# A mixture-of-experts stage: how the rows of each expert are gathered and turned, and which weight loads go first

## The chip, the cores and the metric

The kernel runs on one core of one Trainium2 chip. The core has five engines that run at the same time, each with its own list of instructions: TensorE (PE in the profile; PEld is its weight load), VectorE (DVE), ScalarE (ACT), GpSimd (POOL) and SyncE (SP), which here only issues DMA transfers. The metric is the device time of one execution in microseconds (us); lower is better.

## The reference

One layer of a hybrid encoder block for 512 tokens of width 1024, all in float32. A token mixer (chunked spatial gating beside a gated delta rule) comes first and isn't touched by the change. Then each token goes to 2 of 32 experts, chosen by a router, and each expert is a gated two-layer network:

```
h = _layer_norm(DEEPNORM_ALPHA * h + mix, ln1_g[l], ln1_b[l])
ffn = _hier_moe(h, w_rg[l], b_rg[l], w_re[l], b_re[l], w1[l], w3[l], w2[l])
h = _layer_norm(DEEPNORM_ALPHA * h + ffn, ln2_g[l], ln2_b[l])
...
def expert_block(args):
    xb, e = args
    hb = jax.nn.silu(xb @ w1[e]) * (xb @ w3[e])
    return hb @ w2[e]
```

`w1[e]` and `w3[e]` are 1024 x 512, `w2[e]` is 512 x 1024, so an expert has 6 MB of weights. With 1024 (token, expert) pairs on 32 experts, an expert has 32 rows on average.

## The kernel before, in words

Up to about 690 us of the trace the kernel runs the mixer. Towards its end, normalised rows are written to DRAM in `h1_dram`, two halves of a 128-row tile at a time, by DMAs on ACT's queue (line 978). The router makes for each expert its count of rows (`cnti`) and the list of its tokens (`idx`); the rank of a row is its place in that list. The lists have 160 places (`NB`): ranks 0 to 127 in the first column of `idx`, ranks 128 to 159 in the second (`sort`, line 1086).

From there `Experts.run` (its core stands below) goes through 32 blocks, one for each expert. The order of the work in this stage is written by hand: each engine executes its instructions in the order in which the code emits them.

- **Weights.** `load` issues 1 MB loads on SP's queue (line 395 for the first blocks, line 397 under the condition that the expert has rows): six for each expert, four for the first product and two for the second, 192 in all. They go round through 18 buffers (`raw`). A load waits until the buffer's former contents have been read. 18 loads are issued ahead of the first block; block b then issues four after its first pass and two after the second pass of block b-1.
- **Gathers.** `fetch` (line 1303) has POOL gather the rows of a block from `h1_dram` by two indirect DMAs: 128 rows into one buffer and 32 into another, always both. Two buffers of each kind alternate, and block b+2 is fetched at the start of block b.
- **Turning the rows.** `turn_x` (lines 1314 to 1329) has PE transpose the 128 gathered rows in 8 pieces of 128 columns, four into each of the PSUM banks `t0` and `t1`. ACT (line 1320) and DVE (line 1322) each take four pieces to `x` in SBUF and apply the gain and the bias of the normalisation. Ranks 128 to 159 are transposed (line 1326) only if the count is over 128, into the right half of the bank `yz`; DVE reads them from there in any case (lines 1328 and 1329).
- **First pass.** `up` (line 1342) multiplies x by the first four weight chunks into the bank group `u`: ranks 0 to 31 always in 32 matmuls, ranks 32 to 95 and 96 to 159 each behind a branch on PE with 16 wider ones (the profile counts every matmul in float32 twice, so 64, 96 or 128 for a first pass). `gate` takes silu on ACT (line 1349) and the product on DVE (line 1350) to h.
- **Second pass.** `turn` transposes h through `t1` and `t0` (lines 1356 and 1358; ACT copies them to `hT`, lines 1359 and 1360), and `down` (line 1370) multiplies hT by the last two chunks: ranks 0 to 31 into the left half of `yz`, the others into `y0` and `y1` behind branches. `store_y` copies the results out of PSUM (DVE for `yz`, line 1378; ACT for the others, line 1381) and POOL stores them.

The passes are interleaved: after the first pass of block b, PE transposes the rows of block b+1, runs the second pass of block b-1, and turns h of block b. Pieces of the router's bookkeeping (`more`) are dealt out between these steps. After the blocks come one loop for experts with over 160 rows, which has nothing to do for these inputs, the gather of results for each token, and the last normalisation.

Of the kernel before, what the change touches and what calls it, by code (L numbers as in the profile page):

```python
# [30 lines left out]
NP = 2  # L31
NB = 32 + 64 * NP
NX = 3
# [987 lines left out]
class Router:  # L1021
# [17 lines left out]
    def tile(self, t):  # L1039
# [38 lines left out]
        for i, (a, b) in enumerate(((0, 128), (128, NB))):  # L1078
            for k in range(2):
                nc.tensor.matmul(self.sps[i][0:b - a], oh[:, k, a:b], wt[:, k],  # L1080
                                 start=k == 0 and t == 0, stop=k == 1 and t == NT - 1)

    def sort(self):
        nc, v = self.nc, self.nc.vector
        for i, n in enumerate((128, NB - 128)):
            v.tensor_scalar(self.idx[0:n, i], self.sps[i][0:n], 2.0 * T, None, op0=OP.add)
# [95 lines left out]
    def overflow(self, W, ps, i):  # L1182
# [8 lines left out]
        for h, (a, b) in enumerate(((0, 128), (128, NB))):  # L1191
# [10 lines left out]
class Experts:  # L1202
# [8 lines left out]
    def __init__(self, kk, ctx, cst, land, h1_dram, y_dram):  # L1211
# [8 lines left out]

        self.y0 = ps.tile([128, 512], F32, name="yz")
        self.u = ps.tile([128, NP + 1, 512], F32, name="u")
        self.xt = self.ec(self.tile_pool(name="ext", bufs=2))
# [4 lines left out]
    def clear(self):  # L1228

        for t in [self.u[:, 0:NP], self.y0] + self.y:  # L1230
            self.nc.vector.memset(t, 0.0)

    def run(self, blocks, more=None, clear=None):
# [10 lines left out]
        def load(n):  # L1244
            for _, (b, c) in zip(range(n), todo):
                blk = blocks[b]
                if blk[5] and b not in conds:
# [52 lines left out]
    def fetch(self, b, i):  # L1300

        x = self.land[i][self.nland[i] % 2][0:(128, NB - 128)[i]]
        self.nc.gpsimd.indirect_dma_start(out=x, out_offset=None, in_=self.h1_dram,  # L1303
                                          in_offset=bass.IndirectOffsetOnAxis(ap=self.blocks[b][2 + i], axis=0),
                                          bounds_check=T - 1, oob_is_err=False)
        self.s[b].setdefault("r", []).append(x)
        self.nland[i] += 1

    def turn_x(self, b):

        nc, r, m = self.nc, self.s[b]["r"], NB - 128
        x = self.s[b]["x"] = self.xt.tile([128, KD, NB], F32, name="x")
# [3 lines left out]
        lc = self.kk.lc  # L1316
        for k in range(KD):
            src, lg, lb = self.t[k // 4][:, k % 4 * 128:k % 4 * 128 + 128], lc[:, 0, k:k + 1], lc[:, 1, k:k + 1]
            if k < 4:
                nc.scalar.activation(out=x[:, k, 0:128], in_=src, func=AF.Identity, bias=lb, scale=lg)  # L1320
            else:
                nc.vector.tensor_scalar(x[:, k, 0:128], src, lg, lb, op0=OP.mult, op1=OP.add)
        z = self.y0[:, 256:256 + KD * m]
        with self.tc.If(self.n(b) > 128):
            for k in range(KD):
                nc.tensor.transpose(z[:, k * m:k * m + m], r[1][:, k * 128:k * 128 + 128], self.cst["ident"][0:m, 0:m])
        xh = x[:, :, 128:NB]
        nc.vector.tensor_tensor(out=xh, in0=z.rearrange("p (k n) -> p k n", k=KD), in1=bc(lc[:, 0], m, 2), op=OP.mult)  # L1328
        nc.vector.tensor_tensor(out=xh, in0=xh, in1=bc(lc[:, 1], m, 2), op=OP.add)
# [64 lines left out]
def build(nc, tc, a):  # L1394
# [139 lines left out]
    def dynamic(oi, j):  # L1534
        ids = []

        def srcs():
            if not ids:
# [8 lines left out]
    blocks = [(e * NB, static(e), r.idx[:, 0, e:e + 1], r.idx[0:NB - 128, 1, e:e + 1], r.cnti[0:1, e:e + 1],  # L1547
               i > 3)
# [9 lines left out]
    with tc.For_i(0, nv, 1) as i:  # L1558
# [3 lines left out]
        ex.run([((i + E) * NB, dynamic(so, 0), idx[:, 0:1], idx[0:NB - 128, 1:2], so[0:1, 1, 0:1], False)])  # L1562
# [70 lines left out]
```

## Time and profile before

| what | value |
| --- | --- |
| median of 3 runs | 1276.2 us (1274.17 to 1276.59) |
| the profiled execution, its own time | 1277.76 us |
| its span, first to last instruction | 1276.1 us |
| mean granted clock of PE over the span | 0.951 |
| busy over the span: PE, DVE, ACT, POOL | 1082.8, 634.7, 494.4, 199.9 us |
| DMA traffic over the span | 300.23 MB, 235 GB/s |
| weight loads of the experts | 192 of 1024 KB, 20.6 us from issue to landing |

The busy times are sums over the whole span, of which the stage that the change touches is the part from 700 us on; inside it, a short stretch says more than the sum. A timeline row gives the start, the length, the engine, the line, what is written and read, how often, and in brackets the idle time before it with what ended it. PEclk is the clock granted to PE: 1 is 2.4 GHz, 0.5 is 1.2 GHz.

### The profile page before, as it was taken

The numbers are of one execution on the slowest core, as the hardware profiler recorded it, in microseconds if no ns is written. First come the engines' busy times: TensorE is split into PE (matmuls) and PEld (weight loads), VectorE is DVE, ScalarE is ACT, GpSimd is POOL, SyncE is SP. The second block draws the span as 40 slices with busy tenths as digits, with TensorE's granted clock in tenths as the row PEclk, the third lists the DMA queues.
The fourth block names the chain that finished last, engine by engine and source line by source line (L and its number), as shares of the span: only waits on it lengthen the run. The fifth ranks groups of instructions, "written<-read, shape, count | busy, mean of one in ns | idle before, by whom it ended". The sixth has DMA issues, their size and how long they took to land. (4 is left out here: it accounts for less than half of the span.)

```text
span 1276.1 us, 20920 instructions
## 1 busy us (share of the span) xinstructions
PE 1082.8 (85%) x7782; PEld 716.5 (56%) x7782; DVE 634.7 (50%) x1376; ACT 494.4 (39%) x1039; POOL 199.9 (16%) x367
## 2 busy tenths in 40 slices
PE   4999999999999999999999488878787777789820
PEld 2887788877777777768887234343434333334310
DVE  7475542468777777754764434442223232222256
ACT  6233552445454455445331324332424233222231
POOL 1000110022211212200000202111212212112033
PEclk9999999999999999999989699999999898898965
DMA  4422223699311120114673749999999999999833
GB/s 172 161 66 67 83 83 92 236 371 362 93 51 55 61 67 33 51 52 166 233 280 148 286 190 378 412 416 416 416 417 416 417 416 417 417 417 417 352 107 119
DMA packets 79997, 300.23 MB, mean 235 GB/s; under 512 B 12192, under 2 KB 37024, under 8 KB 55552
## 3 DMA queue, kind: packets, MB, share of 16 engines
q1 hardware_dynamic: 67536, 278.42, 56.6%
q0 software_dynamic: 9744, 15.10, 3.5%
q10 hardware_dynamic: 2592, 4.99, 1.1%
q8 instruction: 86, 1.41, 0.5%
q14 instruction: 39, 0.32, 0.1%
HBM read 285.48 MB, written 50.33 MB: 263 GB/s over the span
## 5 line engine op out<-in xcount | busy, mean ns | idle before, releaser
L1342 PE MATMUL u<-raw,x 128*32 128x256 f32 (+1 forms) x2496 | 226.2, 435 | 14.8 <-DMA raw<-in_w 14.4
L212 PE MATMUL psi<-hTh,hi 128*128 128x512 f32 x456 | 187.9, 414 | 2.2 <-ACT hi L212 2.2
L212 PE MATMUL psi<-hTh,lo 128*128 128x512 f32 x456 | 188.1, 414 | 0.3 <-DVE lo L212 0.3
L212 PE MATMUL psi<-hTl,hi 128*128 128x512 f32 x456 | 186.0, 410 | 0.0
L1350 DVE TENSOR_TENSOR h<-h,u 128x640 f32<-128x640 f32 x32 | 26.3, 821 | 288.8 <-ACT h L1349 288.8
L1342 PEld LDWEIGHTS u<-raw,x 128*32 128x32 f32 (+1 forms) x2496 | 95.8, 118 | 130.5 <-issue 73.2
L212 DVE TENSOR_TENSOR lo<-raw,hi 128x1024 fp32r<-128x1024 f32 x75 | 92.6, 1235 | 65.6 <-ACT hi L212 65.1
L212 ACT CAST hi<-raw 128x1024 fp32r<-128x1024 f32 x75 | 78.4, 1047 | 116.4 <-PE psi L212 103.9
L1370 PE MATMUL yz<-raw,hT 128*32 128x256 f32 x1024 | 69.5, 416 | 59.1 <-DVE x L1328 53.8
L212 PEld LDWEIGHTS psi<-hTh,hi 128*128 128x128 f32 x456 | 86.3, 189 | 21.0 <-ACT hi L212 3.0
L212 PEld LDWEIGHTS psi<-hTh,lo 128*128 128x128 f32 x456 | 86.5, 190 | 18.7 <-issue 3.0
L212 PEld LDWEIGHTS psi<-hTl,hi 128*128 128x128 f32 x456 | 86.3, 190 | 18.1 <-issue 2.7
L1349 ACT ACTIVATE h<-u 128x640 f32<-128x640 f32 x32 | 22.5, 704 | 155.4 <-PEq L1295 111.5
L1370 PEld LDWEIGHTS yz<-raw,hT 128*32 128x32 f32 x1024 | 32.2, 117 | 87.1 <-DVE x L1328 64.9
L1378 DVE COPY ysmall<-yz 32x256 f32<-32x256 f32 x128 | 53.5, 418 | 52.6 <-PE yz L1370 48.7
L1381 ACT COPY ylarge<-y 64x512 f32<-64x512 f32 x128 | 74.3, 580 | 2.8 <-DMA y_dram<-ylarge 1.2
L1359 ACT COPY hT<-t 128x128 f32<-128x128 f32 x32 | 8.5, 265 | 165.0 <-PE t L1356 165.0
L1303 POOL DMA_INDIRECT mh<-h_dram,idx x64 | 63.3, 988 | 49.9 <-issue 13.1
L1387 POOL DMA_DIRECT2D y_dram<-ysmall x32 | 16.0, 501 | 278.0 <-DVE ysmall L1378 266.5
L1314 PE MATMUL t<-ident,mh 128*128 128x128 f32 x256 | 36.0, 286 | 22.6 <-PEq L1295 10.8
L212 DVE SCALAR_TENSOR_TENSOR acc<-xp,cols,acc 128x512 f32<-128x512 f32 x72 | 53.7, 748 | 3.1 <-ACT acc L212 1.9
L1320 ACT ACTIVATE x<-t,lc 128x128 f32<-128x128 f32 x128 | 48.1, 457 | 13.7 <-PE t L1314 11.4
(390 smaller groups left out, 1823.4 us busy)
## 6 DMA issues: line engine op xcount, KB each, us to landing
raw<-in_w SPq DMA_DIRECT2D x192, 1024.0 KB, 20.6
raw<-in_wt SPq DMA_DIRECT2D x73, 512.0 KB, 3.6
y_dram<-zero SPq DMA_DIRECT2D x48, 512.0 KB, 7.2
y_dram<-ylarge POOLq DMA_DIRECT2D x128, 128.0 KB
raw<-in_wv SPq DMA_DIRECT2D x8, 512.0 KB, 7.7
raw<-in_wo SPq DMA_DIRECT2D x4, 1024.0 KB, 7.7
y_dram<-ysmall POOLq DMA_DIRECT2D x32, 128.0 KB
vt<-in_x SPq DMA_DIRECT2D x4, 512.0 KB, 6.1
```

The source lines that it names most:

```text
L212: op._ins = getattr(getattr(self.nc, op.attr), op.name)(*map(real, op.args), **{k: real(x) for k, x in op.kw.items()})
L1303: self.nc.gpsimd.indirect_dma_start(out=x, out_offset=None, in_=self.h1_dram, in_offset=bass.IndirectOffsetOnAxis(ap=self.blocks[b][2 + i] ...
L1314: nc.tensor.transpose(self.t[k // 4][:, k % 4 * 128:k % 4 * 128 + 128], r[0][:, k * 128:k * 128 + 128], self.cst["ident"])
L1320: nc.scalar.activation(out=x[:, k, 0:128], in_=src, func=AF.Identity, bias=lb, scale=lg)
L1342: self.nc.tensor.matmul(self.u[q * r:(q + 1) * r, NP if p is None else p, 0:c], x[:, k, r0:r0 + r], self.raw[b, k // 2][:, o:o + c], start ...
L1349: self.nc.scalar.activation(out=h, in_=u[:, :, 0], func=AF.Silu)
L1350: self.nc.vector.tensor_mul(out=h, in0=h, in1=u[:, :, 1])
L1359: self.nc.scalar.copy(out=x[:, n], in_=self.t[1][:, 0:128])
L1370: self.nc.tensor.matmul(y[q * r:(q + 1) * r, 0:c], t[:, i, j * r:(j + 1) * r], self.raw[b, 4 + k // 2][:, o:o + c], start=k == 0, stop=k == 3)
L1378: nc.vector.tensor_copy(out=small[:, q], in_=self.y0[q * 32:(q + 1) * 32, 0:256])
L1381: nc.scalar.copy(out=large[:, q, p], in_=self.y[p][q * 64:(q + 1) * 64])
L1387: nc.gpsimd.dma_start(out=dst.rearrange("r (q n) -> r q n", q=src.shape[1]), in_=src, cond=c > 32 * j)
```

## The change

The boundary between the two gathers moves from rank 128 to rank 64 (`NA`). Ranks 0 to 63 of each block are gathered always; the second gather, now of 96 rows, stands behind a branch on POOL (count over 64). x lies in two fixed tiles instead of a rotating pool.

In `turn_x`, PE transposes 64 rows in 8 pieces of 64 columns, all into `t0`, and DVE alone takes them to x, in one multiplication and one addition over 512 columns; ACT has no part any more. Ranks 64 to 159 are transposed behind a branch on PE into `t1` (five pieces) and `y1` (three), no longer into `yz`, and DVE takes them to x behind a branch of its own.

In `run`, 13 of the first 18 weight loads are issued ahead of the gathers. The last 5 wait for one-column clears of their buffers on DVE, which stand behind the first gathers and behind the clears of PSUM and x. The first piece of the router's bookkeeping, which makes the counts, comes ahead of the second gathers, since their branches read the counts. The first 18 loads are always made, and all later ones are conditional.

```
+NA = 64
...
-        for i in range(2):
-            for b in range(min(2, nb)):
-                self.fetch(b, i)
-        load(len(kk.raws))
+        late = 5 if clear else 0
+        load(len(kk.raws) - late, True)
+        for b in range(min(2, nb)):
+            self.fetch(b, 0)
+        next(more, None)
+        for b in range(min(2, nb)):
+            self.fetch(b, 1)
         if clear:
             clear()
+
+            for i in range(late):
+                nc.vector.memset(kk.raws[(kk.nraw + i) % len(kk.raws)][:, 0:1], 0.0)
+            load(late, True)
...
+        n = (NA, NB - NA)[i]
+        x = self.land[i][self.nland[i] % 2][0:n]
+        with ExitStack() as st:
+            if i:
+                st.enter_context(self.tc.If(self.n(b, ET.Pool) > NA))
+            self.nc.gpsimd.indirect_dma_start(out=x, out_offset=None, in_=self.h1_dram,
...
+        def affine(rows, parts):
+            for src, k0, k1 in parts:
+                v.tensor_tensor(out=x[:, k0:k1, rows], in0=src.rearrange("p (k n) -> p k n", k=k1 - k0),
+                                in1=bc(lc[:, 0, k0:k1], rows.stop - rows.start, 2), op=OP.mult)
+            v.tensor_tensor(out=x[:, :, rows], in0=x[:, :, rows], in1=bc(lc[:, 1], rows.stop - rows.start, 2), op=OP.add)
...
         for k in range(KD):
-            nc.tensor.transpose(self.t[k // 4][:, k % 4 * 128:k % 4 * 128 + 128], r[0][:, k * 128:k * 128 + 128],
-                                self.cst["ident"])
...
-        z = self.y0[:, 256:256 + KD * m]
-        with self.tc.If(self.n(b) > 128):
-            for k in range(KD):
-                nc.tensor.transpose(z[:, k * m:k * m + m], r[1][:, k * 128:k * 128 + 128], self.cst["ident"][0:m, 0:m])
...
+            nc.tensor.transpose(self.t[0][:, k * NA:k * NA + NA], r[0][:, k * 128:k * 128 + 128], ident[0:NA, 0:NA])
+        affine(slice(0, NA), ((self.t[0], 0, KD),))
+        zs = [(self.t[1][:, 0:k5 * m], 0, k5), (self.y[NP - 1][:, 0:(KD - k5) * m], k5, KD)]
+        with self.tc.If(self.n(b) > NA):
+            for z, k0, k1 in zs:
+                for k in range(k0, k1):
+                    nc.tensor.transpose(z[:, (k - k0) * m:(k - k0 + 1) * m], r[1][:, k * 128:k * 128 + 128], ident[0:m, 0:m])
+        with self.tc.If(self.n(b, ET.DVE) > NA):
+            affine(slice(NA, NB), zs)
```

What this does to the engines' lists is shown at three places. The names are those of the code, with a number behind each; `mh` is a buffer of gathered rows, a wait names the engine or the DMA semaphore waited for.

PE between the first pass of the third block and the second pass of the second, before:

```order
L1314 MATMUL t0_5420<-ident_125,mh_4512 128x128 [waits DMASW4_49,Activation_49]
L1314 MATMUL t0_5420<-ident_125,mh_4512 128x128 x3
L1314 MATMUL t1_5421<-ident_125,mh_4512 128x128 x4
L1287 TENSOR_LOAD cnti_5438
L1324 COMPARE_AND_BRANCH
L1326 MATMUL yz_5424<-ident_125,mh_4512 128x32 [waits DMASW5_49,DVE_49]
L1326 MATMUL yz_5424<-ident_125,mh_4512 128x32 x7
L1324 UNCONDITIONAL_BRANCH
L1324 UNCONDITIONAL_BRANCH [waits PE_49]
L1370 MATMUL yz_5424<-raw3_4854,hT_5639 32x256 [waits DMAHW5_49,DVE_49]
```

The same place after the change:

```order
L1334 MATMUL t0_5420<-ident_125,mh_4512 128x64 [waits DMASW4_49,Activation_49]
L1334 MATMUL t0_5420<-ident_125,mh_4512 128x64 x7
L1295 TENSOR_LOAD cnti_5440
L1337 COMPARE_AND_BRANCH
L1340 MATMUL t1_5421<-ident_125,mh_4512 128x96 [waits DMASW5_49,DMASW2_49]
L1340 MATMUL t1_5421<-ident_125,mh_4512 128x96 x4
L1340 MATMUL y1_5423<-ident_125,mh_4512 128x96 [waits DVE_49]
L1340 MATMUL y1_5423<-ident_125,mh_4512 128x96 x2
L1337 UNCONDITIONAL_BRANCH
L1337 UNCONDITIONAL_BRANCH [waits PE_49]
L1383 MATMUL yz_5424<-raw3_4854,hT_5665 32x256 [waits DMAHW5_49]
```

The transposes are narrower, those behind the branch go to `t1` and `y1`, and the first matmul of the second pass into `yz` has no wait for DVE any more. DVE at the product of a gate and the rows that follow it, before:

```order
L1350 TENSOR_TENSOR h_5913<-h_5913,u_5425 128x640 [waits Activation_49]
L1324 UNCONDITIONAL_BRANCH
L1322 TENSOR_SCALAR x_5916<-t1_5421,lc_4537 128x128 [waits PE_49]
L1322 TENSOR_SCALAR x_5916<-t1_5421,lc_4537 128x128 x3
L1328 TENSOR_TENSOR x_5916<-yz_5424,lc_4537 128x8x32 [waits PE_49]
L1329 TENSOR_TENSOR x_5916<-x_5916,lc_4537 128x8x32 [waits DVE_49]
```

The same place after the change:

```order
L1363 TENSOR_TENSOR h_5941<-h_5941,u_5425 128x640 [waits Activation_49]
L1329 TENSOR_TENSOR x1_5430<-t0_5420,lc_4537 128x8x64 [waits PE_49]
L1331 TENSOR_TENSOR x1_5430<-x1_5430,lc_4537 128x8x64 [waits DVE_49]
L1295 TENSOR_LOAD cnti_5440
L1341 COMPARE_AND_BRANCH
L1329 TENSOR_TENSOR x1_5430<-t1_5421,lc_4537 128x5x96 [waits PE_49]
L1329 TENSOR_TENSOR x1_5430<-y1_5423,lc_4537 128x3x96 [waits PE_49]
L1331 TENSOR_TENSOR x1_5430<-x1_5430,lc_4537 128x8x96 [waits DVE_49]
L1341 UNCONDITIONAL_BRANCH
```

Six instructions on pieces of x have become two, with a load of the count, a branch and three more behind it; the read of `yz` is gone. SP's queue of loads at the start of the stage, before:

```order
L395 DMA raw12_5411<-in_w13 128x2048 [waits DMAHW5_49,PE_49]
L395 DMA raw13_5412<-in_w13 128x2048 [waits DMAHW6_49,PE_49]
L1324 UNCONDITIONAL_BRANCH
L395 DMA raw14_5413<-in_w2 128x2048 [waits DMAHW7_49,PE_49]
L1295 UNCONDITIONAL_BRANCH
L1324 UNCONDITIONAL_BRANCH
L395 DMA raw15_5414<-in_w2 128x2048 [waits DMAHW0_49,PE_49]
L395 DMA raw16_5415<-in_w13 128x2048 [waits DMAHW1_49,PE_49]
L1295 UNCONDITIONAL_BRANCH
L395 DMA raw17_5416<-in_w13 128x2048 [waits DMAHW2_49]
```

The same place after the change:

```order
L396 DMA raw12_5411<-in_w13 128x2048 [waits DMAHW5_49,PE_49]
L1312 UNCONDITIONAL_BRANCH x2
L1337 UNCONDITIONAL_BRANCH
L396 DMA raw13_5412<-in_w13 128x2048 [waits DMAHW6_49,DVE_49,PE_49]
L1341 UNCONDITIONAL_BRANCH
L1312 UNCONDITIONAL_BRANCH
L396 DMA raw14_5413<-in_w2 128x2048 [waits DMAHW7_49,DVE_49,PE_49]
L1303 UNCONDITIONAL_BRANCH
L1337 UNCONDITIONAL_BRANCH
L396 DMA raw15_5414<-in_w2 128x2048 [waits DMAHW0_49,DVE_49,PE_49]
L1312 UNCONDITIONAL_BRANCH
L1341 UNCONDITIONAL_BRANCH
```

The loads into `raw13` to `raw17` have a wait for DVE that they did not have.

## Rows read from the trace of the kernel before

**Rows 1.** Stretches of the core; the first row names the columns.
```profile
core 0: us, PE busy (x) PEld busy (x) DVE busy (x) ACT busy (x) POOL busy (x), PEclk, DMA share, GB/s
718.00:728.00 10.00, 7.26 (x80) 4.72 (x80) 3.09 (x8) 3.21 (x8) 5.20 (x7) 0.74 0.28 62
...
738.00:749.50 11.50, 8.98 (x85) 4.14 (x85) 6.07 (x16) 3.44 (x8) 0.00 (x0) 1.00 0.09 19
...
760.00:1196.00 436.00, 349.42 (x3596) 162.48 (x3597) 135.78 (x336) 145.15 (x305) 79.44 (x190) 0.95 1.01 412
```

**Rows 2.** Waits of SP, 780 to 1186 us: total us, times, longest.
```profile
SPq L397 <- DMA raw<-in_w: 258.2, 129, 3.4
```

**Rows 3.** Timeline of PE, 1085 to 1115 us: start, us, instruction, wait before.
```profile
1097.55 10.23 PE L1342 MATMUL u<-raw,x 128*32 128x256 f32 x48 [1.24 <-DMA raw<-in_w]
```

**Rows 4.** Timeline of PE, 1108 to 1224 us.
```profile
1113.96 17.55 PE L1342 MATMUL u<-raw,x 128*32 128x256 f32 x128
...
1145.41 1.07 PE L1314 MATMUL t<-ident,mh 128*128 128x128 f32 x8 [0.33 <-PEq L1295]
...
1148.46 2.38 PE L1370 MATMUL yz<-raw,hT 128*32 128x256 f32 x32 [1.98 <-DVE x L1328]
...
1164.67 0.68 PE L1326 MATMUL yz<-ident,mh 32*128 32x32 f32 x8
...
1171.09 17.54 PE L1342 MATMUL u<-raw,x 128*32 128x256 f32 x128
...
1219.23 1.93 PE L1370 MATMUL yz<-raw,hT 128*32 128x256 f32 x32 [0.96 <-ACT hT L1360]
```

**Rows 5.** Line 397, the loads: duration ns (min, median, max), starts, and landings.
```profile
L397 SPq DMA_DIRECT2D raw<-in_w x168: 73/333/782, 742.4 to 1185.2; - x168
...
DMA to landing us min/median/max: 4.9/20.8/24.2
```

**Rows 6.** Timeline of all engines, 704.5 to 765 us.
```profile
705.77 1.03 ACTq L978 DMA_DIRECT2D h_dram<-h1s  x2
...
709.53 0.34 DVE L1086 TENSOR_SCALAR idx<-sps 128x32 int32<-128x32 f32 x2 [0.33 <-PE sps L1080]
...
714.01 14.23 SPq L395 DMA_DIRECT2D raw<-in_w  x5
...
716.84 1.28 POOL L1303 DMA_INDIRECT mh<-h_dram,idx  x1 [12.14 <-DMA h_dram<-h1s]
```

**Rows 7.** Line 978, the stores of rows, 700 to 720 us: landings.
```profile
DMA to landing us min/median/max: 9.4/9.4/9.4
```

**Rows 8.** Line 978, 655 to 685 us: landings of an earlier tile's stores.
```profile
DMA to landing us min/median/max: 2.0/2.2/2.5
```

**Rows 9.** Timeline of PE, 718 to 775 us.
```profile
719.65 1.94 PE L1314 MATMUL t<-ident,mh 128*128 128x128 f32 x8 [9.99 <-DMA mh<-h_dram,idx]
...
721.89 4.25 PE L1342 MATMUL u<-raw,x 128*32 128x256 f32 x64 [0.30 <-PEq L1324]
...
729.88 12.36 PE L1342 MATMUL u<-raw,x 128*32 128x256 f32 x96
...
742.79 1.06 PE L1314 MATMUL t<-ident,mh 128*128 128x128 f32 x8 [0.55 <-PEq L1295]
...
748.43 10.68 PE L1342 MATMUL u<-raw,x 128*32 128x256 f32 x96
...
769.15 3.66 PE L1342 MATMUL u<-raw,x 128*32 128x256 f32 x64
```

**Rows 10.** Groups by line, 715 to 1222 us: busy us, mean ns, idle before.
```profile
L1350 DVE TENSOR_TENSOR h<-h,u 128x640 f32<-128x640 f32 x32 | 26.3, 821 | 288.8 <-ACT h L1349 288.8
...
L1328 DVE TENSOR_TENSOR x<-yz,lc 128x256 f32<-128x256 f32 x32 | 13.2, 412 | 0.0
```

**Rows 11.** Waits of PE, 715 to 1222 us.
```profile
PE yz L1370 <- DVE x L1328: 53.8, 28, 2.2
```

**Rows 12.** Timeline of ACT, 1144 to 1152 us.
```profile
1145.24 0.70 ACT L1349 ACTIVATE h<-u 128x640 f32<-128x640 f32 x1 [0.86 <-PEq L1295]
```

More of the change, by code (lines that the diff above doesn't have):

```diff
@@ L1077, in tile @@
         v.tensor_tensor(out=oh, in0=bc(cst["iota"], 2, 1), in1=bc(rk, NB, 2), op=OP.is_equal)
-        for i, (a, b) in enumerate(((0, 128), (128, NB))):
+        for i, (a, b) in enumerate(((0, NA), (NA, NB))):
             for k in range(2):
@@ L1084, in sort @@
         nc, v = self.nc, self.nc.vector
-        for i, n in enumerate((128, NB - 128)):
+        for i, n in enumerate((NA, NB - NA)):
             v.tensor_scalar(self.idx[0:n, i], self.sps[i][0:n], 2.0 * T, None, op0=OP.add)
@@ L1190, in overflow @@
         idx = W.tile([128, 2], I32, name="ofx")
-        for h, (a, b) in enumerate(((0, 128), (128, NB))):
+        for h, (a, b) in enumerate(((0, NA), (NA, NB))):
             for k in range(2):
@@ L1222, in __init__ @@
         self.u = ps.tile([128, NP + 1, 512], F32, name="u")
-        self.xt = self.ec(self.tile_pool(name="ext", bufs=2))
+        xt = self.ec(self.tile_pool(name="ext", bufs=1))
+        self.x = [xt.tile([128, KD, NB], F32, name="x%d" % i) for i in range(2)]
         self.hp = self.ec(self.tile_pool(name="ehp", bufs=1))
@@ L1228, in clear @@
     def clear(self):
-        for t in [self.u[:, 0:NP], self.y0] + self.y:
+        for t in [self.u[:, 0:NP]] + self.y + [x[:, :, NA:96] for x in self.x]:
             self.nc.vector.memset(t, 0.0)
@@ L1242, in run, with load @@
         conds, self.raw, todo = {}, {}, iter(steps)
-        def load(n):
+        def load(n, always=False):
             for _, (b, c) in zip(range(n), todo):
                 blk = blocks[b]
-                if blk[5] and b not in conds:
+                if blk[5] and not always and b not in conds:
                     m = nc.values_load(blk[4], engines=(ET.SP,), min_val=-T, max_val=T,
@@ L1300, in fetch @@
     def fetch(self, b, i):
[L1302 to L1305, printed above, removed]
+        n = (NA, NB - NA)[i]
[4 more added lines that the diff above has]
+            self.nc.gpsimd.indirect_dma_start(out=x, out_offset=None, in_=self.h1_dram,
+                                              in_offset=bass.IndirectOffsetOnAxis(ap=self.blocks[b][2 + i], axis=0),
+                                              bounds_check=T - 1, oob_is_err=False)
         self.s[b].setdefault("r", []).append(x)
@@ L1323, in turn_x @@
-        z = self.y0[:, 256:256 + KD * m]
-        with self.tc.If(self.n(b) > 128):
-            for k in range(KD):
-                nc.tensor.transpose(z[:, k * m:k * m + m], r[1][:, k * 128:k * 128 + 128], self.cst["ident"][0:m, 0:m])
-        xh = x[:, :, 128:NB]
-        nc.vector.tensor_tensor(out=xh, in0=z.rearrange("p (k n) -> p k n", k=KD), in1=bc(lc[:, 0], m, 2), op=OP.mult)
-        nc.vector.tensor_tensor(out=xh, in0=xh, in1=bc(lc[:, 1], m, 2), op=OP.add)
+        nc, v, r, lc, m, ident = self.nc, self.nc.vector, self.s[b]["r"], self.kk.lc, NB - NA, self.cst["ident"]
@@ L1561, in build @@
         idx = r.overflow(C, ex.t, i)
-        ex.run([((i + E) * NB, dynamic(so, 0), idx[:, 0:1], idx[0:NB - 128, 1:2], so[0:1, 1, 0:1], False)])
+        ex.run([((i + E) * NB, dynamic(so, 0), idx[0:NA, 0:1], idx[0:NB - NA, 1:2], so[0:1, 1, 0:1], False)])
     kk.finish(RS, r, y_dram)
```

14 lines of the change are left out of this document (4 added, 10 removed).

## The prediction, made before the change was run

> **What bounds the kernel now.** I read the stretches first, then who waits for whom, then the timeline of TensorE (PE) around the places that the change touches. From 760 to 1196 us the share of the DMA engines is 1.01 at 412 GB/s [rows 1]. In that stage the 1 MB weight loads are the bound, and the queue of loads waits mostly for earlier loads: 258.2 us in 129 waits [rows 2]. Work that PE saves there is worth nothing by itself. The two ends of the stage look different. Before it the DMA engines stand idle: share 0.09 from 738 to 749.5 [rows 1], because all 18 weight buffers are full and wait for PE. After it PE is late: its last wait for a weight ends at 1097.55 [rows 3], and from there it runs without one to 1219.23 + 1.93 = 1221.16 [rows 4]. The last load is issued at 1185.2 and lands by the median 20.8 us later [rows 5], near 1206. So time is won in two ways only: PE frees its first buffers earlier, which moves the whole stream, or PE needs less time between its last starvation and its end. The two add, as the stream between them is rigid. What follows PE's end is a chain of stores, gathers and the last normalisation, about 55 us of the span, and the change doesn't touch it.
>
> **The first gather.** The last two stores of normalised rows to DRAM are issued at 705.77 to 706.8 [rows 6]. They take 9.4 us to land [rows 7], while the pair of an earlier tile took 2.0 to 2.5 us [rows 8] with no weight load under way. The gather that waits for them starts at 716.84 [rows 6]. Four of the five loads that are moved were issued ahead of those stores, so their 4 MB are what the stores lie behind; the fifth is at 714.01 [rows 6]. Without them the stores land at about 709.0. Next late is then the gather's index list, ready at 709.53 + 0.34 = 709.87 [rows 6]. The gather starts at 709.9, 6.9 us earlier. From gather to transposes it was 719.65 - 716.84 = 2.81 us [rows 6, 9], so they start at 712.7. Eight transposes of 64 columns aren't in the trace: 0.68 us for eight of 32 columns [rows 4] and 1.06 us for eight of 128 (at 742.79 [rows 9]) bound them at full clock, 1.94 us [rows 9] at half. I take 1.3 us for these cold ones, nearest to the middle, and 0.8 us later. VectorE (DVE) then does both passes over x: 0.412 us for 256 elements and 0.821 for 640 [rows 10] give 1.07 ns each, so 0.69 us for 512, 1.4 for two. DVE's own list ahead of them (index, clears, five one-column clears) I count at 4.0 us, to 713.9, just in time; half a microsecond more would show. The first matmuls start at 715.6 instead of 721.89 [rows 9].
>
> **The late loads.** They wait for the five one-column clears, at about 713.5. The first lands 4.9 us later at the earliest [rows 5], the fifth by some 729 at 2.5 us per MB. The first of them is needed by the third expert's first pass, near 739. The price is nothing while those 10 us or more of cover stand, and a microsecond for each beyond them. 11 idle microseconds of DMA move from 738-749.5 to 703-714.
>
> The Trainium skill speaks against this step: "DMA: Bandwidth & Descriptors", Rules for kernel authors, says to issue a DMA early and wait for it late. By that rule alone the sum would lose those 11 us. The row at 738 [rows 1] disagrees: loads that were early filled the buffers and then stood.
>
> **From expert to expert.** After each first pass PE transposes the next expert's rows, and then the second pass waits for DVE's read of the bank yz: 53.8 us in 28 waits [rows 11]. Example: a first pass ends at 1145.41 - 0.33 = 1145.08, the second starts at 1148.46 [rows 4], 3.38 us. The changed transposes use other banks, so the second pass no longer waits for that read. What is left is the branch (0.33), eight transposes (0.8) and another branch (0.30, as at 721.89 [rows 9]): 1.43 us, 1.95 less. Where the next expert has over 64 rows, eight transposes of 96 columns come on top (0.68 to 1.06, I take 0.95). New waits: the transposes of h now wait for DVE to pass its branch. DVE ends x about 3.1 us after the first pass (ScalarE starts 0.16 after it and takes 0.70 [rows 12], then 0.82 + 0.69 + 0.69 on DVE); load and branch add 0 (overlapped) to 0.9 us (three of PE's branches). PE comes there at 1.43 + 1.93 [rows 4] and a hand-over, 3.5. I take no wait, and up to 0.5 us per gap for the range. Where the next expert has over 64 rows DVE goes on: passes of 480, 288 and 768 elements, at the same rate 0.65 + 0.45 + 0.96 = 2.1, so it ends near 5.5, and PE comes at 3.5 + 0.95 = 4.5. There the wait is 1.0, and with the 0.95 nothing is left of the 1.95. ScalarE loses four passes that aren't on the path, and GpSimd's branches lie beside it.
>
> **The sum.** First expert's first pass: 64 matmuls, 3.66 us at 2.4 GHz [rows 9], up to twice that at 1.2 GHz; PE was granted 1.2 GHz until within that pass (mean share 0.74 from 718 to 728 [rows 1], and 4.25 us for the pass), and will start colder. I take 5.7, so it ends at 721.3 instead of 726.14, 4.8 us earlier. Gap to the next: 3.74, now 3.1 (no second pass stands in it yet). The second expert's pass took 12.36 us, partly at 1.2 GHz, against 10.68 for the same work [rows 9]; I take 11.0: 735.4 instead of 742.24, 6.8 earlier. Then two gaps of 1.95: 8.8 earlier at 759.11 and 10.7 at 772.81 [rows 9]. There the next loads go out, the first that lands into an unbroken stream. The stream moves by **10.7 us** (8 to 12: the clock of the first two passes). In the tail, six gaps: 4 x 1.95 and 2 x 0, **7.8 us** (5 to 12; spells at 1.2 GHz in it may go or come). The two gaps are those ahead of the long passes at 1113.96 and 1171.09, 128 matmuls each [rows 4]. Together 18.5. There is room for it: the last weights would land near 1195, and PE's last second pass, at 1219.23 now, would start near 1200.7. The stream would still not end last. Profiled: 1277.76 - 18.5 = 1259.3; this execution was 1.56 above the median of the runs, so against the median 1276.2 - 18.5 = **1257.7 us**.
>
> **Rivals.** (1) The stores don't wait behind the loads. Then the gather starts as late as before and the start gains only its gaps, 0.6 + 2 x 1.95 = 4.5: 1276.2 - 4.5 - 7.8 = 1263.9. Against it: 9.4 us with loads, 2.5 without. For it: the loads that stay are in the same queue, and some of the delay may be theirs. The Trainium skill's page "DMA: Bandwidth & Descriptors", Queues, rings and completion order, says each DMA engine takes turns between its queues, packet by packet; by that rule a store from another queue would hardly wait, and this rival would hold. The 9.4 us [rows 7] say otherwise.
> (2) DVE becomes the bound between experts. It now makes x alone, in line after the gate's product, with a load from memory and a branch behind it. If that ends 1 us late, each gap keeps 0.95: start 6.8 + 2 x 0.95 = 8.7, tail 4 x 0.95 = 3.8, less 1 in each of the two others, together 10.5: 1265.7. For it: the margin is 0.3 us.
> (3) Slower: a skipped gather on GpSimd waits for the landing of an earlier transfer of its semaphore before it passes. Stores of results stand behind it, their single buffer holds DVE's copy, and that holds PE's second pass in the bank yz. In the stream's stage it hides. In the tail, with up to 9.4 us (the slowest landing above) in five gaps, it costs up to 47 us. It decides once wait and stores together pass the 8 us of a short expert (3.66 + 1.43 + 1.93 and the transposes of h), and the kernel is slower where that leaves over 18.5 / 5 = 3.7 us in each: at 6 us, 1257.7 + 30 = 1287.7. Against it: the transfer waited for is several back.
> (4) The late loads hold PE. From 10 us of lateness on, each costs one; the case for it is the rule above: 1257.7 + 11 = 1268.7.
>
> **How the numbers follow.** Forecast 0.64 (1250 to 1262), rival 1 0.12, rival 2 0.11, rival 4 0.04, rival 3 0.06, and 0.03 for a change that does nothing that counts. The range 1250 to 1268 takes in the forecast and rivals 1 and 2 with 2 us beyond them, and leaves out about 0.16. A measurement of this kernel can tell 0.2%, 2.6 us. Faster 0.89 (the forecast, rivals 1 and 2, and half of rival 4), same 0.04, slower 0.07.
>
> **What would show it.** First gather near 710 and first matmul of the experts near 715.6; DMA share near 0 from 703 to 714 and no hole of 11 us at 738; the stream unbroken from about 765; the wait of the second pass for DVE gone from PE's list; gaps of 1.4 us in the tail, and PE's end near 1203. I would be wrong if the gather still starts after 714, if the transposes of h wait for DVE in most gaps, if GpSimd's stores come late, or if PE waits for weights after the first experts and the stream shows a new hole.

## The result: 8 us faster, where 18.5 were forecast

| | before | changed | forecast |
| --- | --- | --- | --- |
| median | 1275.58 us (1274.17 to 1276.59) | 1267.49 us (1265.38 to 1272.44) | 1257.7 us (1250 to 1268) |

The ratio of the changed kernel to the one before is 0.9945, with a 95% interval of 0.9923 to 0.9966. The direction was right and the time lies just inside the range, but less than half of the gain came. The profiled execution of the changed kernel took 1272.44 us, the slowest of its six, with a span of 1270.8 us.

### What happened as forecast

The first group is the timeline of all engines from 704.5 to 716 us, beside [rows 6]: start, length, engine, line, what is written and read, and in brackets the wait before.

```profile
705.06 1.03 ACTq L979 DMA_DIRECT2D h_dram<-h1s  x2
709.44 0.46 DVE L1087 TENSOR_SCALAR idx<-sps 64x32 int32<-64x32 f32 x2 [0.29 <-PE sps L1081]
709.93 1.22 POOL L1315 DMA_INDIRECT mh<-h_dram,idx  x1 [5.94 <-DVE idx L1087]
...
713.00 2.79 SPq L396 DMA_DIRECT2D raw<-in_w  x5
```

The first gather starts at 709.93 (forecast 709.9), and what it waits for is the index list, no longer the stores of rows. (Counted from those stores, which go out 0.71 us earlier here than in [rows 6], the gather is 0.74 us later than forecast; that the two times agree to 0.03 us is in part luck.) The five late loads go out at 713.00 (forecast 713.5). PE, in its timeline from 712 to 765 us, beside [rows 9]:

```profile
712.56 1.08 PE L1334 MATMUL t<-ident,mh 64*128 64x64 f32 x8 [2.89 <-DMA mh<-h_dram,idx]
715.16 6.46 PE L1355 MATMUL u<-raw,x 128*32 128x256 f32 x64 [1.51 <-DVE x L1331]
...
724.78 0.47 PE L1369 MATMUL t<-ident,h 128*128 128x128 f32 x1 [2.30 <-DVEq L1341]
...
726.04 11.48 PE L1355 MATMUL u<-raw,x 128*32 128x256 f32 x96
...
760.81 3.66 PE L1355 MATMUL u<-raw,x 128*32 128x256 f32 x64
```

The first pass starts at 715.16 (forecast 715.6), and the fourth one ends at 764.47 where it ended at 772.81 before: 8.3 us earlier. Of these, 0.7 us are that this execution comes to the stage earlier; counted from the stores of rows it is 59.41 us instead of 67.04, so 7.6 us earlier, a little under the forecast 8 to 12 (a second profile, below, has the forecast 10.7). PE's waits from 712 to 1216 us (total, times, longest) show that the wait of [rows 11], 53.8 us for DVE's read of the bank yz, is gone:

```profile
PE u L1355 <- DMA raw<-in_w: 29.8, 24, 3.1
PE t L1369 <- PEq L1303: 14.4, 26, 1.8
PE t L1334 <- PEq L1303: 12.5, 27, 2.3
PE yz L1383 <- DMA raw<-in_w: 11.9, 8, 2.3
...
PE t L1369 <- DVEq L1341: 2.8, 3, 2.3
```

DVE's new branch is waited for three times in all, 2.8 us. What has grown is the wait for weights: 29.8 + 11.9 us, where PE's waits from 712 to 1222 us before have

```profile
PE u L1342 <- DMA raw<-in_w: 14.4, 10, 3.0
...
PE yz L1370 <- DMA raw<-in_w: 4.0, 2, 2.0
```

By itself this growth doesn't show a slower stream: a PE that needs less time waits longer for the same stream. The kernel with gathers of 128 and 32 rows, below, whose stream has its old rate, also waits 33.7 us in these two rows.

### What did not

Stretches of the changed kernel, with the columns of [rows 1] (busy time of PE, PEld, DVE, ACT and POOL, then PE's granted clock, the DMA share and GB/s):

```profile
718.00:728.00 10.00, 7.51 (x77) 3.95 (x73) 3.29 (x11) 1.56 (x3) 0.94 (x1) 0.69 1.02 394
...
738.00:749.50 11.50, 10.99 (x129) 5.69 (x131) 5.59 (x11) 3.43 (x7) 1.67 (x6) 1.00 0.06 14
...
760.00:1190.00 430.00, 353.13 (x3596) 163.03 (x3600) 120.89 (x228) 104.36 (x194) 58.12 (x169) 0.91 1.01 402
```

In the long stretch the DMA engines are as busy as before (share 1.01) and move less: 402 GB/s instead of 412 [rows 1]. The row from 738 shows a sign of the prediction that failed: it had said that no hole would be left there, and the DMA engines still stand at a share of 0.06 and 14 GB/s. From 703 to 714 their share did fall, from 1.01 to 0.21. The hole stayed because the change also left out four loads of the fourth expert, which has no rows; a run below makes them again. The loads, by line (duration ns, starts, landings):

```profile
L398 SPq DMA_DIRECT2D raw<-in_w x174: 73/337/404, 721.8 to 1187.8; - x174
...
DMA to landing us min/median/max: 5.2/20.8/26.8
```

The last one is issued at 1187.8, against 1185.2 before [rows 5]. The stream began 8.3 us earlier and ended 2.6 us later: 10.9 us were lost inside it.

Where they were lost shows in steps of 2 us. These are the steps behind the gathers for the 15th expert, which has over 96 rows (gathers issued at 884.01 and 885.30 in the changed kernel):

```profile
886.00:888.00 2.00, 0.32 (x9) 0.05 (x1) 1.54 (x5) 0.00 (x0) 0.30 (x1) 1.00 1.04 426
888.00:890.00 2.00, 1.72 (x21) 0.90 (x21) 0.25 (x1) 1.46 (x4) 0.54 (x1) 1.00 1.04 313
890.00:892.00 2.00, 0.77 (x16) 0.42 (x16) 0.00 (x0) 1.72 (x3) 0.14 (x3) 1.00 1.00 281
892.00:894.00 2.00, 0.30 (x8) 0.00 (x0) 0.00 (x0) 0.00 (x0) 0.91 (x2) 1.00 1.00 322
894.00:896.00 2.00, 0.63 (x8) 0.40 (x12) 0.00 (x0) 0.00 (x0) 0.10 (x1) 0.74 1.04 428
```

And the same in the kernel before (gathers at 899.65 and 901.01):

```profile
901.50:903.50 2.00, 1.70 (x32) 0.94 (x32) 0.67 (x2) 0.00 (x0) 0.46 (x1) 1.00 1.04 424
903.50:905.50 2.00, 1.82 (x32) 1.11 (x29) 1.66 (x4) 1.08 (x3) 0.00 (x0) 1.00 0.98 406
905.50:907.50 2.00, 2.00 (x44) 1.23 (x40) 0.01 (x1) 1.95 (x4) 0.63 (x3) 1.00 1.02 422
```

From 888 to 894 the engines are as busy as ever and move 281 to 322 GB/s instead of over 400. Each packet takes longer: in the trace's records of packets, the 8 KB packets of the weight loads took between 374 and 486 ns in the mean of each of these six microseconds, and about 313 ns elsewhere. Such spells stand 4 us behind nearly every gather of the changed kernel that brings more than a few rows, the long ones behind the six gathers of 96 rows; behind those of the kernel before there is a single one, of 1.5 us, at 805 us. Over the stream (747 to 1212 us) the mean 8 KB packet took 325.2 ns, and 316.1 before (755 to 1210). Over 20,736 packets on 16 engines the difference is 20,736 x 9.1 ns / 16 = 11.8 us, near the 10.9 that the stream lost.

### The profile page after: what moved, and what is told of

The parts are those of the page before. It is cut to its first block, busy times and chain, and to the rows that moved or that the text cites. A ratio compares the mean times of both kernels' runs of the same rounds, so it can differ in the third digit from the quotient of the medians.

```text
span 1270.8 us, 20916 instructions
## 1 busy us (share of the span) xinstructions
PE 1091.1 (86%) x7822; PEld 717.5 (56%) x7822; DVE 621.4 (49%) x1272; ACT 447.4 (35%) x911; POOL 172.9 (14%) x341
## 3 DMA queue, kind: packets, MB, share of 16 engines
q0 software_dynamic: 6832, 15.09, 3.6%
## 5 line engine op out<-in xcount | busy, mean ns | idle before, releaser
L1355 PE MATMUL u<-raw,x 128*32 128x256 f32 (+1 forms) x2496 | 236.9, 448 | 33.1 <-DMA raw<-in_w 29.8
L1383 PE MATMUL yz<-raw,hT 128*32 128x256 f32 x1024 | 73.5, 423 | 22.8 <-DMA raw<-in_w 11.9
L1383 PEld LDWEIGHTS yz<-raw,hT 128*32 128x32 f32 x1024 | 37.1, 118 | 46.6 <-issue 19.5
L1383 PE MATMUL y<-raw,hT 128*64 128x512 f32 x224 | 51.6, 608 | 0.0
L1315 POOL DMA_INDIRECT mh<-h_dram,idx x38 | 37.3, 982 | 42.5 <-PE t L1334 9.4
L1334 PEld LDWEIGHTS t<-ident,mh 64*128 64x128 f32 x256 | 19.7, 148 | 35.4 <-issue 32.4
```

Of the source, the lines that this page charges most:

```text
L1334: nc.tensor.transpose(self.t[0][:, k * NA:k * NA + NA], r[0][:, k * 128:k * 128 + 128], ident[0:NA, 0:NA])
L1355: self.nc.tensor.matmul(self.u[q * r:(q + 1) * r, NP if p is None else p, 0:c], x[:, k, r0:r0 + r], self.raw[b, k // 2][:, o:o + c], start ...
L1383: self.nc.tensor.matmul(y[q * r:(q + 1) * r, 0:c], t[:, i, j * r:(j + 1) * r], self.raw[b, 4 + k // 2][:, o:o + c], start=k == 0, stop=k == 3)
```

## The experiments

The theory: **the shape of the gathers costs the time**. While the rows of a gather of 64 or 96 rows move, every weight packet beside them is slower, and the stream of loads, which bounds the stage, is longer by that. The rivals: that execution was disturbed; something else in the change (the order, the branches, the late loads) slows the packets; or a term of the forecast's sum is wrong. Ten runs were made, the first of them of the changed kernel as it stands. The medians, and two measures of the stream: GB/s from 780 to 1160 us in the profiled execution, and the mean time of an 8 KB packet of the weight loads over the stream.

| kernel | median us | ratio to before (95%) | GB/s | ns |
| --- | --- | --- | --- | --- |
| before | 1274.45 to 1275.58 | 1 | 416 | 316.1 |
| changed, second time | 1265.29 | 0.9925 (0.9907 to 0.9944) | 404 | 325.0 |
| changed, gathers of 128 and 32 rows | 1254.80 | 0.9841 (0.9827 to 0.9856) | 416 | 316.3 |
| before, two gathers of 64 rows for 128 | 1285.29 | 1.0080 (1.0065 to 1.0094) | 402 | 327.0 |
| changed, no late loads | 1273.57 | 0.9987 (0.9976 to 0.9998) | 403 | 324.8 |
| before, with the late loads | 1267.75 | 0.9945 (0.9928 to 0.9961) | 416 | 316.4 |
| changed, 128 and 32 rows, no late loads | 1260.41 | 0.9879 (0.9860 to 0.9897) | 416 | 316.4 |
| changed, 64 rows always, 128 and 32 behind the branch | 1267.12 | 0.9931 (0.9915 to 0.9948) | 406 | 322.9 |
| changed, gathers of 112 and 48 rows | 1266.00 | 0.9926 (0.9910 to 0.9942) | 405 | 323.8 |
| as the third, loads of the first four experts unconditional | 1256.32 | 0.9854 (0.9834 to 0.9874) | 416 | 316.2 |
| as the third, 9 late loads | 1252.35 | 0.9827 (0.9807 to 0.9846) | 417 | 316.3 |

### The changed kernel a second time

No edit.

> The changed kernel a second time, for a second profile. In the first one the 8 KB packets of the weight loads took 400 to 530 ns instead of 313 in spells that began 4 us after the issue of a gather, while the gather's own rows moved. Theory (the shape of the gathers, 64 and 96 rows instead of 128, slows the weight packets beside them): the same spells again, the six longest behind the six gathers of 96 rows, mean over the stream about 325 ns, time 1265 to 1270 us. Rival (that execution was disturbed by something else): the spells are elsewhere or gone, mean near 316 ns as in the kernel before.

Median 1265.29 us; the spells stand again behind the gathers, the long ones at 825 to 831, 885 to 891, 938 to 945, 1000 to 1005, 1077 to 1084 and 1142 to 1149 us, 1 to 4 us ahead of where they were, as its whole stage is. The first profile was no accident in that.

In another way it was not typical. PE's timeline of this second profile from 712 to 765 us, and the stretch from 718 to 728:

```profile
714.56 5.16 PE L1355 MATMUL u<-raw,x 128*32 128x256 f32 x64 [1.51 <-DVE x L1331]
...
723.59 10.68 PE L1355 MATMUL u<-raw,x 128*32 128x256 f32 x96
...
757.55 3.66 PE L1355 MATMUL u<-raw,x 128*32 128x256 f32 x64
```

```profile
718.00:728.00 10.00, 7.51 (x113) 4.14 (x107) 3.29 (x11) 1.56 (x3) 0.93 (x1) 1.00 1.01 390
```

From 718 to 728 us PE was granted its full clock here (1.00, against 0.69 in the first profile), and the first two passes took 5.16 and 10.68 us instead of 6.46 and 11.48. The fourth first pass ends at 761.21, 56.37 us behind the stores of rows at 704.84: 10.7 us earlier than before, which is the forecast.

### Gathers of 128 and 32 rows in the changed kernel

```
...
-        n = (NA, NB - NA)[i]
+        n = (128, NB - 128)[i]
...
-        zs = [(self.t[1][:, 0:k5 * m], 0, k5), (self.y[NP - 1][:, 0:(KD - k5) * m], k5, KD)]
+        zs = [(self.t[1], NA, 128), (self.y[NP - 1][:, 0:KD * (NB - 128)], 128, NB)]
...
+            for (z, n0, n1), src, i0 in zip(zs, (r[0][NA:128], r[1]), (NA, 0)):
...
```

The router's lists are cut at rank 128 as in the kernel before. Still 64 rows are turned always and the rest behind the branches; where they lie differs, and that those behind the branch take 16 transposes instead of 8.

> The changed kernel, but ranks 0 to 127 come by one gather of 128 rows, always, and ranks 128 to 159 by one of 32 behind the branch; which rows are turned always (64) and which behind a branch (96), the banks, the order and the late loads stay as in the changed kernel. Theory (the shape of the gather): spells gone, packets back at 316 ns, stream at 412 GB/s, last weight load issued near 1176 instead of 1187.8, time 1256 to 1260 us, which is what was predicted for the change. Rival (disturbed execution, or the order of the work): spells stay, 1265 to 1270 us.

Median 1254.80 us, 10.5 under the changed kernel of the same set of runs and a little under what the theory expected. The stream is back at the rate of the kernel before (first row), and the steps behind the gathers for the 15th expert, issued here at 874.59 and 875.95, have no hole:

```profile
780.00:1160.00 380.00, 319.21 (x3262) 147.23 (x3256) 104.64 (x198) 91.30 (x169) 55.06 (x153) 0.92 1.02 416
```

```profile
876.50:878.50 2.00, 1.20 (x17) 0.57 (x18) 0.44 (x2) 0.00 (x0) 0.38 (x1) 1.00 1.02 422
878.50:880.50 2.00, 0.81 (x9) 0.57 (x11) 1.44 (x4) 1.19 (x3) 0.23 (x1) 1.00 0.98 408
880.50:882.50 2.00, 1.03 (x16) 0.45 (x11) 0.00 (x0) 1.95 (x4) 0.40 (x3) 1.00 1.06 428
```

The last load is issued at 1169.6 instead of 1187.8, and PE ends at 1193.32 instead of 1213.48:

```profile
L398 SPq DMA_DIRECT2D raw<-in_w x174: 73/337/682, 718.4 to 1169.6; - x174
```

(1.9 us of these differences are not the gather's: the executions differ in when the stage begins, here by 703.18 for the last stores of rows against 705.06 in the changed kernel.) Counted from these stores the fourth first pass ends 56.27 us on, 10.8 us earlier than before.

### The other way round: two gathers of 64 rows in the kernel before

```
...
-        self.nc.gpsimd.indirect_dma_start(out=x, out_offset=None, in_=self.h1_dram,
...
+        for o, ix in zip((x[0:64], x[64:128]) if i == 0 else (x,), idx if i == 0 else (idx,)):
+            self.nc.gpsimd.indirect_dma_start(out=o, out_offset=None, in_=self.h1_dram,
...
```

> The kernel before, but its gather of 128 rows is split into two of 64 rows, ranks 0 to 63 into partitions 0 to 63 and ranks 64 to 127 into partitions 64 to 127; same rows, same bytes, one more small instruction for the second list and one more issue for each block. Theory (the shape): spells behind the gathers here too, mean packet about 325 ns; the stream ends up to 12 us later, of which PE's slack at the end hides a part, so 1278 to 1285 us. Rival (something else in the change slows the packets): 316 ns and 1276 us, or 1 us more for the issues.

Median 1285.29 us, 10.8 us slower than the kernel before, with spells behind the gathers and a mean packet of 327.0 ns. The stretch of the stream, and two steps behind the gathers issued from 902.40 on:

```profile
780.00:1160.00 380.00, 301.18 (x3034) 140.95 (x3032) 112.53 (x277) 126.67 (x264) 89.21 (x191) 0.91 1.02 402
```

```profile
908.00:910.00 2.00, 2.00 (x44) 1.21 (x40) 0.59 (x2) 1.96 (x4) 0.62 (x3) 1.00 1.00 289
910.00:912.00 2.00, 1.33 (x28) 0.52 (x16) 0.00 (x0) 1.13 (x3) 0.09 (x2) 1.00 1.11 287
```

The same rows and bytes in another shape cost what the changed kernel lost. The time is 0.3 us above the expected range, which is within the noise. This kernel has one gather more for each block; that the number of gathers isn't what counts is seen at 112 rows below, where it is that of the kernel with 128 and 32.

### Without the late loads

```
-        late = 5 if clear else 0
+        late = 0
```

> The changed kernel with all first 18 loads ahead of the gathers, as before. Theory of the prediction (stores of rows lie behind the loads, 9.4 instead of 2 us): stores land near 715.5, first gather near 716.8, first matmul of the experts near 722 instead of 715.16, the stream starts 5 to 6.5 us later, 1271 to 1274 us. Rival (the moved loads are not what the stores wait for, or what they cost and gain cancels): gather near 710 and 1267 us.

Median 1273.57 us, 8.3 over the changed kernel of the same runs. The timeline of all engines from 700 to 724 us:

```profile
704.80 1.03 ACTq L979 DMA_DIRECT2D h_dram<-h1s  x2
...
715.75 1.22 POOL L1315 DMA_INDIRECT mh<-h_dram,idx  x1 [12.03 <-DMA h_dram<-h1s]
```

With all loads ahead of them the stores again keep the gather waiting, for 12.03 us. That is the step of the prediction. How the stores lose the time stands in the trace's records of packets. In the kernel before, the first of their 256 packets of 2 KB starts at 709.34, 3.6 us behind the issue (0.8 in the changed kernel, without loads), and the last at 715.34. From 709 to 714 us, 205 packets of the stores and 198 of the loads start: one for one. The Trainium skill's page "DMA: Bandwidth & Descriptors", Queues, rings and completion order, says that each DMA engine takes turns between its queues, packet by packet, and these records agree. A packet of a load took 315 ns in that time and one of a store 84, so 256 / 16 = 16 packets of the stores on each engine, each with a load's packet before it, take about 16 x 0.4 = 6.4 us by estimate; measured 6.0. So the prediction read the rule wrongly, when it took from it that a store would hardly wait: the 9.4 us do not speak against taking turns. Where the first 3.6 us come from was not seen.

### The late loads alone, in the kernel before

```
...
-        load(len(kk.raws))
+        late = 5 if clear else 0
+        load(len(kk.raws) - late)
...
+            load(late)
...
```

> The kernel before with one part of the change: 13 loads ahead of the gathers, the last 5 behind the one-column clears. Theory of the prediction: the stores of rows land by 709, the first gather starts near 710 instead of 716.8, everything after it is 6 to 7 us earlier and the stream runs at 412 GB/s as before: 1267 to 1269 us against 1274.5. Rival (late loads hold PE later on, and the gain is given back): 1272 to 1275 us.

Median 1267.75 us, 7.35 under the kernel before; 6.9 us were worked out from the stores and the index list. The timeline of all engines from 700 to 724 us, and the stretch that stood empty in [rows 1]:

```profile
702.00 1.03 ACTq L978 DMA_DIRECT2D h_dram<-h1s  x2
...
706.70 1.28 POOL L1307 DMA_INDIRECT mh<-h_dram,idx  x1 [5.78 <-DVE idx L1086]
```

```profile
738.00:749.50 11.50, 10.96 (x101) 4.58 (x94) 1.63 (x4) 3.37 (x6) 2.71 (x7) 1.00 0.55 196
```

The stream keeps its 416 GB/s. So the late loads are not what slows the packets, and the gain isn't given back.

### The new way of turning rows alone

The kernel with gathers of 128 and 32 rows, with `late = 0`.

> The changed kernel with gathers of 128 and 32 rows and with all first 18 loads ahead of the gathers: what the new way of turning rows is worth alone. Theory (start and gaps add): 1254.8 plus 6 to 8.5 us, 1261 to 1263 us, which is 11 to 13 us under the kernel before. Rival (the two hide behind each other): 1255 to 1258 us.

Median 1260.41 us, 14.7 under the kernel before, and 5.6 over the one with late loads. So turning is worth 14.7 us alone (with what else the change has beside the late loads and the shape of the gathers, the left-out loads and the order of the bookkeeping) and the late loads 7.35, 22.0 in sum, and 1274.49 - 1254.80 = 19.7 together: the two parts do add, less 2.3 us, which is about what one such ratio leaves open (0.2%).

### How the loss is shared

```
...
-            self.nc.gpsimd.indirect_dma_start(out=x, out_offset=None, in_=self.h1_dram,
...
+            for o, p in ((x, ix[2]), (self.s[b]["r"][0][NA:96], ix[3])) if i else ((x[0:NA], ix[2][0:NA]),):
+                self.nc.gpsimd.indirect_dma_start(out=o, out_offset=None, in_=self.h1_dram,
...
```

> The changed kernel with the gather of 64 rows always, but behind the branch one of 128 rows and one of 32 instead of one of 96. It tells how the loss is shared. Theory (each row of a gather of 64 or 96 rows slows the weights beside it): spells behind the 64-row gathers stay, about half of the loss, mean packet about 320 ns, 1258 to 1262 us. Rival (the loss is that of the 96-row gathers): 316 to 317 ns and 1255 to 1256 us.

Median 1267.12 us, 5 us above what was expected. The time can't answer the question, because the experiment moves more: behind the branch it fetches up to 64 rows again, some 390 packets of 4 KB, 1.6 MB or 3.9 us at 412 GB/s. The packets answer it: 322.9 ns, so three quarters of the difference, 322.9 - 316.3 of 325.0 - 316.3 ns, are there without any gather of 96 rows. In the spells of this kernel the packets are slow while the 64 rows move (470 to 490 ns in the microseconds from 883 and 884) and back at 312 to 318 ns while those of the 128-row gather do (886 to 889).

### 112 rows

Against the kernel with gathers of 128 and 32 rows:

```
...
-        n = (128, NB - 128)[i]
+        n = (112, NB - 112)[i]
...
```

> The changed kernel with gathers of 112 rows (always) and 48 (behind the branch). 112 rows land in partitions of both halves, 64 don't. Theory A (only a gather of all 128 rows leaves the weights alone, since its rows are dealt to the DMA engines in the same way as those of a weight load): spells stay, 1262 to 1267 us. Theory B (what matters is that the landing buffer reaches partitions 64 and up): spells gone behind the always-made gathers, 316 to 318 ns, 1255 to 1257 us.

Median 1266.00 us and 323.8 ns, with spells at all the six places, and shorter ones (346 to 405 ns, from 816 to 820 us) behind 112-row gathers that no gather of 48 follows:

```profile
780.00:1160.00 380.00, 311.94 (x3229) 144.65 (x3227) 106.74 (x205) 91.56 (x170) 53.56 (x151) 0.91 1.02 405
```

Theory A holds as far as time goes: a landing buffer that reaches into the upper partitions doesn't help, only the full 128 rows did. The Trainium skill bears on both theories. The Trainium skill's page "SBUF — State Buffer", Door 1, says that partitions 0 to 63 are reached by 8 of the 16 ports and 0 to 127 by all of them. If all that counted were that a gather reaches into both halves of the partitions, 112 rows would be as harmless as 128, and the 405 GB/s disagree. The Trainium skill's page "DMA: Bandwidth & Descriptors", The descriptor swizzle, says that in a transfer to 128 partitions each DMA engine writes the partitions of one port, and gives no such map for other shapes. If with fewer rows one engine writes into the port of another, the engines would meet there; that is a guess which the trace allows, with 128 rows clean and 64, 96 and 112 not. No run shows which engine wrote which row, so the mechanism is open, and only the shape is shown.

### Two things that the prediction had left out or put a price on

The condition of the first four experts' loads, undone in the kernel with gathers of 128 and 32 rows:

```
-               True)
+               i > 3)
```

> The changed kernel with gathers of 128 and 32 rows, with one part of the change undone that the prediction did not cost: the loads of the first four experts are always made again. The fourth expert has no rows, so the change left out 4 of its 6 loads. Theory (they lay where the buffers were full and the DMA engines idle, so they are worth nothing): 1254 to 1256 us, as with the loads left out. Rival (4 MB of the stream at 2.5 us each): 1263 to 1265 us, and the gain would be theirs in good part.

Median 1256.32 us against 1254.80 in an earlier set, intervals overlapping: the 4 MB of an expert without rows, which the change leaves out, are worth little or nothing. They lay in the stretch with idle DMA engines, which is filled again here (0.06 in the changed kernel):

```profile
738.00:749.50 11.50, 11.16 (x127) 5.39 (x127) 5.30 (x11) 3.07 (x6) 1.75 (x6) 1.00 0.63 237
```

So it is the left-out loads that kept the hole at 738 open.

More late loads:

```
-        late = 5 if clear else 0
+        late = 9 if clear else 0
```

> The changed kernel with gathers of 128 and 32 rows and 9 late loads instead of 5. Theory (with 5 the stores of rows land in 2 us already, and the late loads have cover): 1253 to 1256 us, no difference. Rival (late loads hold PE, the fourth rival of the prediction): the second expert's first pass waits for weights, 2 to 8 us more, 1257 to 1263 us.

Median 1252.35 us, no slower, and perhaps 2 us faster than with 5, which runs from different sets can't settle. The fourth rival, late loads that hold PE, is out for 9 of them as well. This is the fastest kernel measured here, 1.7% under the kernel before.

## Why the prediction was wrong, step by step

**What bounds the kernel, and the first gather:** right. The stream bounded the middle, time was to be had at its two ends, and the gather waits for the index list, as forecast, 0.03 us from its time by the luck told above. The late loads alone brought 7.35 us for 6.9. The ground given for the first rival was wrong, though: the stores do take turns with the loads, one packet for one, and the greater part of their lateness is that (6.0 us to move instead of 2.0). "No hole at 738" was wrong too: the loads that the change leaves out were not in the sum.

**The start of the stream:** right in size. Counted from the stores of rows it was 7.6 us in the first profile, whose first two passes took 0.8 and 0.5 us more than assumed at the low clock told above, and 10.7 and 10.8 us in the second and in the kernel with gathers of 128 rows, for 10.7. One of its terms was mis-sized: the gap behind the first expert's first pass was taken as 3.1 us and measured 726.04 - 721.62 = 4.4, and 723.59 - 719.72 = 3.9 in the second profile. The 3.1 is when DVE is done; the transposes of h with their hand-over come behind it. In the second profile the two passes were 0.5 and 0.3 us shorter than assumed, which made up for it.

**"The two add, as the stream between them is rigid":** this is the step that failed. It took the rate of the stream as given, though the change touches what else is on the DMA engines. The gather of 64 rows was costed as a wait at the start (2.81 us from gather to transposes) and as an issue on GpSimd, never as packets beside the weights: its rows were the same rows, and the trace of before held no gather of another count in the stream with many rows to move. The transposes of a new width got bounds from both sides; for the rate of the stream beside gathers of a new shape none was set. What the runs showed in its place: the 8 KB packets went from 316 to 325 ns, the stream from 416 to 404 GB/s at the same share, and the price was 10.5 us with late loads (1265.29 against 1254.80) and 13.2 without (1273.57 against 1260.41).

**The tail:** the mechanism was right, and the size of the gaps a little too small. It shows undisturbed in the kernel with gathers of 128 and 32 rows. PE's timeline from 1092 to 1195 us there, beside [rows 4]:

```profile
1127.75 1.93 PE L1383 MATMUL yz<-raw,hT 128*32 128x256 f32 x32 [0.37 <-PEq L1336]
1129.62 7.09 PE L1383 MATMUL y<-raw,hT 128*64 128x512 f32 x32
...
1141.86 0.70 PE L1340 MATMUL t<-ident,mh 64*128 64x64 f32 x8
...
1143.10 1.93 PE L1383 MATMUL yz<-raw,hT 128*32 128x256 f32 x32
1145.21 0.30 PE L1369 MATMUL t<-ident,h 128*128 128x128 f32 x1 [0.18 <-PEq L1303]
...
1191.39 1.93 PE L1383 MATMUL yz<-raw,hT 128*32 128x256 f32 x32 [0.31 <-issue]
```

The gap ahead of the second pass at 1127.75 is 1127.75 - 1126.37 = 1.38 us, against 1.43 forecast and 3.38 before. The wide gap, 1140.99 to 1143.10, is 2.11, and the transposes of h follow at 1145.21 without a wait for DVE: 1.27 us were gained there where the forecast had put nothing. From the first pass of the 27th expert to PE's end it was 1221.16 - 1113.96 = 107.2 us before and 1193.32 - 1097.58 = 95.7 there, 11.5 less where 7.8 were forecast. Not all of it is the change's. In the profile of before, two second passes of this stretch ran at a lower clock (0.84 from 1148.46 to 1159.00 and 0.52 from 1166.72 to 1170.30, against 1.00 in the kernel with gathers of 128 rows). From its timeline of PE, behind the row at 1148.46 [rows 4]:

```profile
1150.77 8.29 PE L1370 MATMUL y<-raw,hT 128*64 128x512 f32 x32
...
1166.72 3.54 PE L1370 MATMUL yz<-raw,hT 128*32 128x256 f32 x32 [1.37 <-DVE x L1328]
```

With the 2.38 us of that row, and beside 1.93, 7.09 and 1.93, these are 3.3 us more, so that some 8 to 9 us are left for the gaps. In the changed kernel itself it was 1213.48 - 1112.15 = 101.3: the late stream ate half, since PE was waiting for weights again in its 30th expert.

**What follows PE's end** was put at an unchanged 55 us. It was 1270.8 - 1213.48 = 57.3 against 1276.1 - 1221.16 = 54.9, and 56.8 in the kernel with gathers of 128 rows. What makes these 2 us or so wasn't tried.

**The rivals:** none of them was it. The first (stores that don't wait) and the second (DVE as the bound) would each have given a time near the measured one, 1263.9 and 1265.7, and both are refuted by the rows above: 709.93 for the gather, 2.8 us in three waits for DVE. The third would have cost PE up to 47 us; PE's waits hold nothing of that size but the wait for weights. The fourth is out by the runs with late loads. A time inside the range said nothing on the reasons.

With the one step mended, by giving the gather its 128 rows back, the sum comes out near: forecast 18.5 us, measured 1274.49 - 1254.80 = 19.7. That is the sum and not each term: the profiles give 10.8 us at the start, 8 to 9 in the gaps of the tail, and some 2 us back behind PE's end.

## What to carry to other kernels

Where transfers bound a stage, ask of every change what it does to the other traffic on the DMA engines, their shapes included, and watch GB/s at an unchanged share of busy time: a share of 1.0 doesn't say that the rate is the same. Trimming a gather to the rows in use saved no bytes here (GpSimd's queue moved 15.09 MB, and 15.10 before, with 3,680 packets of 4 KB in both), since rows beyond the count had not been fetched, and cost 10 us. And loads that are issued early into buffers that will only stand full are worth holding back behind a small store that something waits for.

## What the runs showed of the hardware that was not expected

- Rows of an indirect gather into 64, 96 or 112 partitions slow the 8 KB packets of loads on another queue from about 313 to between 340 and 560 ns (means of a microsecond) while they move, at an unchanged busy share; those of a gather into 128 partitions don't (310 to 325 ns).
- A stream of 1 MB loads and a small store on different queues take turns packet for packet, 205 to 198 in 5 us, and so not byte for byte, since a packet of the store has 2 KB and one of the loads 8 KB: the store took 9.4 us to land behind the loads [rows 7], and 2.0 to 3.0 us without them ([rows 8], and 3.0 in the kernel before with late loads).
- One execution differs from another by up to 4.7 us in the stages ahead of the change (the last stores of rows go out between 702.00 and 706.69 in the twelve profiles), so that two profiles should be compared from a common event and not from the span's start.
